# A hybrid attention and state-space layer: who requests the copies of V and the raw weights, and how far apart the convolution and SSD steps stand

## The chip, the cores and the metric

The kernel runs on one core of one Trainium2 chip. The metric is the device time of one execution in microseconds; two runs of the kernel before gave 2359.36 and 2364.16 us, median 2361.76.

## The reference

One decoder layer over 2048 tokens of width 1024, in float32. A projection gives queries, keys, values and a gate for attention, and a gate, an input and the matrices B and C for a state-space mixer:

```python
proj = jnp.einsum('bsd,de->bse', x, w_in[layer])
q, k, v, z_att, z_ssm, xbc, dt_raw = jnp.split(proj, list(SPLITS), axis=-1)
...
o1, l1 = dilated_window_attention(q, k, v, slopes, DILATIONS[0])
o2, l2 = dilated_window_attention(q, k, v, slopes, DILATIONS[1])
o3, l3 = dilated_window_attention(q, k, v, slopes, DILATIONS[2])
...
xbc = jax.nn.silu(causal_depthwise_conv(xbc, conv_w[layer], conv_b[layer]))
xs, bm, cm = jnp.split(xbc, [D_SSM, D_SSM + SSM_GROUPS * SSM_STATE], axis=-1)
...
mix = jnp.concatenate([y_att, y_ssm], axis=-1)
out = jnp.einsum('bse,ed->bsd', mix, w_out[layer])
x = layer_norm(alpha * x + out, ln_g[layer], ln_b[layer])
```

Attention has 16 heads and runs with dilations 1, 4 and 16, so the keys' and values' positions are wanted in three orders. The mixer (SSD) works in 16 chunks of 128 tokens and two groups of heads, so in 32 units, with a causal convolution of width 4 ahead of it and a Silu behind that.

## The kernel before, in words

The engines are called PE (TensorE, matmul), DVE (VectorE), ACT (ScalarE), POOL (GpSimd) and SP (SyncE). SP, ACT and POOL request DMA transfers, each in its own order; a request that has to wait holds up everything behind it on that engine. Matrices are split into a high and a low float32r part, and a product is three matmuls.

**Stage 1, to about 207 us.** V (and the raw time step dt) is computed from `xT`; the rows go to DRAM as `d_v[0]` (`v_out`, L163), dt as `d_dt` (L214). Meanwhile POOL loads the first token side T, 14 tiles of 1 MB.

**Stage 2, 207 to about 1421 us.** All other projections, 44 jobs of two column blocks each. A job is a Strassen-like scheme of seven products (`products`, L283), in the order of the T tiles B11, T1, B21, T2, B22, T4, T3. A product is 12 matmuls into one PSUM bank. ACT evicts four of the seven with `keep` (L297), DVE adds the others to them with `put` (L303, L305). The first ten jobs work on the first half of the tokens (phase 0), the next 22 on the second half (phase 1), the last 12 on the first again (phase 2); at each change all T tiles are loaded anew by POOL (L229). The kinds are c (convolution input), s (SSD gate), q, k and z.

A job's seven weight tiles come from four raw blocks: `column_load` (L234) requests four loads of 256 KB into `wr` tiles (seven buffers), and `column_side` (L241) makes the sums on DVE (L244) and splits each into high (ACT, L248) and low (POOL, L249). The load is requested by POOL, at the seventh step of the job two before the one that uses it; the split runs one job ahead, from its third step on, so that a weight tile is ready five products before it is used.

**What sets the order.** PE, DVE, ACT and POOL follow the program's text. `after(n, f)` puts a piece of work n steps later, and `flush` runs the pieces of a step; a step is one product. SP's order is not the text's: a scheduler sets it from its own estimate of when each request could go.

Pieces that the change touches:

- `copy_v` (L475, request in L478): 32 copies of 512 KB from DRAM to DRAM that write V in the orders of dilations 4 (`d_v[1]`) and 16 (`d_v[2]`). They are entered for every fourth step from step 3 on; attention reads the result from 1421 us on.
- `sums_load` and `sums_part` (L95, L103): in the first four jobs, `xT` is loaded again (L100), DVE and ACT make the sums T1 to T4 of the second token half (L108, L110, L111), and SP stores them (L112). The `to` tiles have two buffers.
- `decays` (L422): loads dt back in 16 small requests (`xr`, L433) and computes the decays, a chain of small operations.
- `conv_tiles` (L370) sets up the two tiles U of a convolution job: SP loads, and a small memset on POOL (L378) that has to wait until the tile's former contents are stored. `conv_fin` (L382) places the five steps of each convolution (`conv_steps`, L390): a scaling on ACT (L395), three taps on DVE (L398), and four Silu pieces on ACT (L404), after which SP stores the result. The first convolution of a job has its steps at 5 to 9, the second at 10 to 14, counted from the job's first step.
- `ssd_load` (L485) and `ssd1` to `ssd5`: per unit, ACT requests `xs`, `bc` and `csb`, two steps ahead of the unit; `ssd5` ends with the gating, and for the first four chunks with a split of the result (L578, L579). `spots` gives each unit its step, every five steps at first and then about every four. `ssd_plan` (L609) enters them all at the first step of job 22.

**Stage 3, from 1421 us.** Attention, then the output projection and the layer norm.

Of the kernel before, what the change touches and what calls it, by code (L numbers as in the profile page):

```python
# [9 lines left out]
F32 = mybir.dt.float32  # L10
# [7 lines left out]
D = 1024  # L18
NR = 16
NJ = 128  # L20
# [8 lines left out]
def hybrid_layer(ctx, tc, xT, xc, w52, wv, convw, convb, dtb, alog, dskp, gcol, wout,  # L29
# [56 lines left out]
    with ExitStack() as c1:  # L86
# [147 lines left out]
        def column_load(ct0, ct1):  # L234

            q = {nm: wr.tile([128, 4, 128], F32, name="wr") for nm in ("S1", "A11", "A12", "A22", "A21")}
            for nm, ct, h in (("A21", ct1, 0), ("A22", ct1, 1), ("A11", ct0, 0), ("A12", ct0, 1)):
                nc.gpsimd.dma_start(q[nm], w52[ct][:, 4 * h:4 * h + 4, :])
            return q
# [130 lines left out]
        def conv_tiles(i):  # L370
            U = []
            for ci in range(2):
                u = cp.tile([128, 19, NJ], F32, name="U", bufs=2)
                for tb in range(2):
                    nc.sync.dma_start(u[:, 3 + tb:19:4, :],
                                      d_cu[i + ci][:, tb].rearrange("p (s j) -> p s j", j=NJ))
                nc.sync.dma_start(u[:, 0, 1:NJ], d_cu[i + ci][:, 1, 3 * NJ:4 * NJ - 1])
                nc.gpsimd.memset(u[:, 0:3, 0:1], 0.0)  # L378
                U.append(u)
            return U  # L380

        def conv_fin(i, U):  # L382
            def f(ci, q, e):
                nc.vector.tensor_copy(U[ci][:, 1 + q, 1:NJ], U[ci][:, 17 + q, 0:NJ - 1])
                if (ci, q) in ((1, 0), (0, 1)):
                    for n, g in enumerate(conv_steps(U[ci], i + ci)):
                        after(n + 3 * ci, g)
            return f
# [86 lines left out]
        def copy_v(d, b):  # L475

            o = (b % 4 * 512 + b // 4 * 32, 8 * b)[d - 1]
            nc.sync.dma_start(d_v[d][b], dap(d_v[0], o * D, [[128 * D, (4, 16)[d - 1]], [D, (32, 8)[d - 1]], [1, D]]))  # L478
# [82 lines left out]
        def ssd5(A):  # L561
# [34 lines left out]
        q = column_load(*cts[0])  # L596
# [7 lines left out]
        q = column_load(*cts[1])  # L604
        units = [(n, g) for n in range(16) for g in range(2)]
        spots = [7 * 22 + 5 + 5 * i if i < 13 else 7 * 32 + (41 * (i - 13)) // 10 for i in range(32)]
        SSD, global_q, sd, H = {}, [None], None, None

        def ssd_plan():  # L609
# [16 lines left out]
        with tc.manual_schedule(engines={E.PE, E.DVE, E.Activation, E.Pool}):  # L626
# [13 lines left out]
            for m, (ph, (kind, i)) in enumerate(jobs):  # L640
# [33 lines left out]
                if m == 22:  # L674
                    after(0, ssd_plan)
# [6 lines left out]
                W, T, q = nW, nT, global_q[0]  # L682
# [536 lines left out]
```

## Time and profile before

| | |
|---|---|
| median of the two runs | 2361.76 us |
| the profiled execution | 2359.14 us, span 2357.3 us, mean granted clock 0.939 |
| PE busy | 2076.8 us, 88% |
| DVE, ACT, POOL busy | 1363.4, 1133.8, 1057.4 us |
| DMA | 557.5 MB, 237 GB/s in the mean |
| POOL on raw weight loads (L238) | 128 requests, 69.1 us |
| ACT waiting for the loads of `csb` (L511) | 69.4 us |

How to read it. Busy PE time says little where matmuls run at half pace, so the granted clock stands beside it, and the time of a stage is compared with the number of its matmuls. "A <- B" means that A sat idle until B ended. A bracket behind a timeline row is the idle time ahead of it and who ended it. SPq, ACTq and POOLq are the requests of DMA transfers; an "issue" as a releaser is time in which the profile shows no cause. All times of a timeline are microseconds from the span's start.

### The profile page before, as it was taken

What the parts mean: (1) busy time and instruction counts of PE and PEld (TensorE: products, weight loads), DVE (VectorE), ACT (ScalarE), POOL (GpSimd) and SP (SyncE); (2) the same over time, 40 slices, a digit from 0 to 9 for tenths busy, and PEclk for the clock granted to TensorE, in tenths of its full rate; (3) what the DMA queues carried; (4) which work ended last, traced back from release to release, by engine and by line L of the source; (5) the groups of instructions that cost most, each with busy time, mean ns of one, the idle gap of its engine ahead of it and who ended that gap; (6) DMA issues with size and microseconds to landing.
All of it is one profiled execution on the core that took longest, in us unless ns stands there. A gap on an engine that the chain in (4) does not pass through costs nothing.

```text
span 2357.3 us, 38953 instructions
## 1 busy us (share of the span) xinstructions
PE 2076.8 (88%) x13824; PEld 1721.2 (73%) x13824; DVE 1363.4 (58%) x3141; ACT 1133.8 (48%) x2969; POOL 1057.4 (45%) x935
## 2 busy tenths in 40 slices
PE   7997148997999788997899997999999996899998
PEld 7997037876777566775678875888788885788886
DVE  3521026435677756773445543888888883666555
ACT  3321025433445456673466644888788882122221
POOL 2122025554556556774444423277666663222221
PEclk9998579999999999998999995999999998899999
DMA  9997376695546788999989984477777779532220
GB/s 334 376 326 300 139 252 216 223 341 199 150 128 213 266 304 318 347 334 390 358 275 303 322 268 160 138 213 221 219 216 228 231 232 315 188 122 89 85 87 35
DMA packets 272882, 557.51 MB, mean 237 GB/s; under 512 B 45360, under 2 KB 136624, under 8 KB 256688
## 3 DMA queue, kind: packets, MB, share of 16 engines
q1 hardware_dynamic: 207200, 308.59, 40.3%
q0 software_dynamic: 44752, 204.49, 24.6%
q10 hardware_dynamic: 20736, 41.95, 5.7%
q8 instruction: 109, 1.79, 0.3%
q14 instruction: 85, 0.70, 0.1%
HBM read 357.42 MB, written 214.30 MB: 243 GB/s over the span
## 4 chain that ended last, share of the span: by engine, by line
PE 41%; DMA 10%; DVE 4%; ACT 3%; issue 1%; POOL 1%; SPq 0%; ACTq 0%; POOLq 0%; DVEq 0%
PE S L785 5%; PE N L834 5%; PE T L814 5%; PE S L994 3%; PE S L996 3%; PE S L995 3%; PE pp L288 3%; PE pp L290 3%; PE pp L292 3%; ACT P L801 2%; PE T L994 2%; DMA bc<-d_bc 2%; PE T L995 2%; PE T L996 2%; DMA kl<-d_kl 1%; DMA wb<-d_wd 1%
## 5 line engine op out<-in xcount | busy, mean ns | idle before, releaser
L249 POOL TENSOR_TENSOR w<-wr,w 128x512 fp32r<-128x512 f32 x224 | 330.9, 1491 | 314.1 <-ACT w L248 310.1
L801 ACT ACTIVATE P<-P,st 128x256 f32<-128x256 f32 (+1 forms) x768 | 345.1, 451 | 96.2 <-DVE st L793 95.5
L793 DVE CUSTOM_DVE_ANT_0 P<-S,tb 128x256 f32<-128x256 f32 (+1 forms) x768 | 235.1, 362 | 98.7 <-PE S L785 66.5
L816 DVE COPY PT<-T 128x512 f32<-128x512 f32 (+1 forms) x304 | 196.5, 677 | 1.5 <-PE T L814 1.5
L297 ACT COPY ev<-pp 128x512 f32<-128x512 f32 x176 | 102.4, 582 | 182.8 <-PE pp L292 145.8
L814 PE MATMUL T<-ident,P 128*128 128x128 f32 x1200 | 179.5, 287 | 5.9 <-DVE PT L816 5.9
L248 ACT CAST w<-wr 128x512 fp32r<-128x512 f32 x224 | 136.5, 619 | 93.6 <-DMA wr<-w 49.3
L834 PE MATMUL N<-PT,v 128*64 128x128 f32 x2400 | 176.6, 284 | 0.0
L244 DVE TENSOR_TENSOR wr<-wr 128x512 f32<-128x512 f32 x128 | 134.5, 1051 | 51.8 <-DMA wr<-w 31.6
L305 DVE TENSOR_TENSOR ev<-pp,ev 128x512 f32<-128x512 f32 x152 | 100.7, 682 | 92.4 <-PE pp L292 72.6
L834 PEld LDWEIGHTS N<-PT,v 128*64 128x64 f32 x2400 | 129.3, 138 | 33.3 <-issue 22.6
L814 PEld LDWEIGHTS T<-ident,P 128*128 128x128 f32 x1200 | 130.0, 142 | 30.8 <-DVE PT L816 7.3
L288 PE MATMUL pp<-TT3h,w 128*128 128x512 f32 x176 | 73.6, 418 | 83.1 <-ACT ev L297 83.0
L801 ACT ACTIVATION_READ_ACCUMULATOR P<-P,st 128x1 f32 x768 | 143.8, 187 | 0.0
L901 POOL TENSOR_TENSOR wb<-num,wb 128x2048 f32<-128x2048 f32 x21 | 96.4, 4591 | 97.0 <-DMA wb<-d_wd 83.6
L785 PE MATMUL S<-kh,qp 64*128 64x256 f32 (+1 forms) x1024 | 126.5, 306 | 0.0
L971 DVE TENSOR_REDUCE tb<-P 128x128 f32<-128x1024 f32 x32 | 64.0, 1999 | 84.9 <-PE N L1000 49.2
L511 ACT ACTIVATE mt<-csb,cs 128x128 f32<-128x128 f32 x256 | 78.4, 390 | 70.7 <-DMA csb<-d_cs 69.4
L345 DVE SCALAR_TENSOR_TENSOR ev<-ev 128x512 f32<-128x512 f32 x64 | 64.0, 1015 | 77.2 <-ACT ev L344 77.2
L288 PE MATMUL pp<-TB22h,w 128*128 128x512 f32 x176 | 77.0, 437 | 35.5 <-ACT ev L297 35.4
L785 PEld LDWEIGHTS S<-kh,qp 64*128 64x128 f32 x1024 | 88.9, 188 | 22.0 <-issue 21.0
L288 PEld LDWEIGHTS pp<-TT3h,w 128*128 128x128 f32 x176 | 34.8, 197 | 95.1 <-ACT ev L297 87.3
(362 smaller groups left out, 6110.5 us busy)
## 6 DMA issues: line engine op xcount, KB each, us to landing
d_wc<-w SPq DMA_DIRECT2D x84, 512.0 KB
w<-d_wc POOLq DMA_DIRECT2D x84, 512.0 KB, 7.4
wr<-w POOLq DMA_DIRECT2D x128, 256.0 KB, 4.9
v<-d_v POOLq DMA_DIRECT2D x24, 1024.0 KB, 7.0
wb<-d_wd SPq DMA_DIRECT2D x48, 512.0 KB
csb<-d_cs ACTq DMA_DIRECT2D x32, 512.0 KB
st<-xT SPq DMA_DIRECT2D x31, 512.0 KB
d_v<-vt SPq DMA_DIRECT2D x16, 512.0 KB
```

What stands on the lines that cost most here:

```text
L244: tt = lambda o, a, b, op=OP.subtract: nc.vector.tensor_tensor(q[o], q[a], q[b], op=op)
L248: nc.scalar.copy(t[:, 0], q[nm])
L249: nc.gpsimd.tensor_tensor(t[:, 1], q[nm], t[:, 0].bitcast(F32), op=OP.subtract)
L288: nc.tensor.matmul(ps, w[:, 0, k], th[:, k], start=start and k == 0, stop=False, skip_group_check=not start)
L785: nc.tensor.matmul(ov(sp[h][:, 256 * b:256 * b + w]), A["q"][d][x][hr, blk], kv(A["k"][y][hr]), start=(m == 0), stop=(m == 2))
L793: nc.vector.tensor_tensor_reduce(P[:, h, b, 256 - w:256], sp[h][:, c0:c0 + w], tab[:, h, tab.shape[2] - w:], 1.0, 3.0e38, OP.add, OP.min, ...
L801: nc.scalar.activation(p, p, AF.Exp, bias=stat(A, 0, d, h, blk), scale=-1.0, accum_out=stat(A, 1, d, h, blk))
L814: nc.tensor.transpose(tp[:, h, b], P[:, h, b, 128 * which:128 * which + 128], ident)
L816: nc.vector.tensor_copy(pt[:, :, bl[0]:2], tp[:, :, bl[0]:2])
L834: nc.tensor.matmul(nm[64 * h:64 * h + 64, bq * 128:bq * 128 + 128], v[:, k, 64 * h:64 * h + 64], pts[which][:, h, b], start=(f or not whic ...
L994: nc.tensor.matmul(ps, uh[:, e, :], wh, start=(e == 0), stop=False)
L995: nc.tensor.matmul(ps, uh[:, e, :], wl, start=False, stop=False)
```

## The change

1. `copy_v` is requested by ACT instead of SP, so that it stands where the text puts it.
2. `column_load` inside the loop over jobs (30 jobs, 120 requests) is requested by ACT instead of POOL, and in four pieces, at steps 3, 4, 6 and 7 of the job, in the order A11, A12, A22, A21, instead of all four at step 6 in the order A21, A22, A11, A12. The loads of the first two jobs stay on POOL.
3. Each convolution's Silu stands two steps behind its last tap instead of one, and the second convolution's steps stand at 11, 12, 13, 14 and 16. The second U tile of a job is set up three steps after the first.
4. The SSD units start two steps later, at a spacing of 63/13 of a step instead of 5 for the first 13; their loads stand three steps ahead of the unit instead of two; the split of the first chunks' result becomes a step of its own (`ssd6`), one later. `ssd_plan` is entered three steps later.

```diff
-        def column_load(ct0, ct1):
-
-            q = {nm: wr.tile([128, 4, 128], F32, name="wr") for nm in ("S1", "A11", "A12", "A22", "A21")}
-            for nm, ct, h in (("A21", ct1, 0), ("A22", ct1, 1), ("A11", ct0, 0), ("A12", ct0, 1)):
-                nc.gpsimd.dma_start(q[nm], w52[ct][:, 4 * h:4 * h + 4, :])
-            return q
+        def column_load(ct0, ct1, queue=nc.gpsimd):
+
+            q = {}
+
+            def load(nm, ct, h):
+                q[nm] = wr.tile([128, 4, 128], F32, name="wr")
+                queue.dma_start(q[nm], w52[ct][:, 4 * h:4 * h + 4, :])
+
+            def first():
+                q["S1"] = wr.tile([128, 4, 128], F32, name="wr")
+                load("A11", ct0, 0)
+            return q, [first, lambda: load("A12", ct0, 1), lambda: load("A22", ct1, 1), lambda: load("A21", ct1, 0)]
...
-        def conv_tiles(i):
-            U = []
-            for ci in range(2):
-                u = cp.tile([128, 19, NJ], F32, name="U", bufs=2)
...
+        def conv_tile(i, U):
+            u = cp.tile([128, 19, NJ], F32, name="U", bufs=2)
...
-                        after(n + 3 * ci, g)
+                        after((0, 1, 2, 3, 5)[n] + 4 * ci, g)
...
-            nc.sync.dma_start(d_v[d][b], dap(d_v[0], o * D, [[128 * D, (4, 16)[d - 1]], [D, (32, 8)[d - 1]], [1, D]]))
+            nc.scalar.dma_start(d_v[d][b], dap(d_v[0], o * D, [[128 * D, (4, 16)[d - 1]], [D, (32, 8)[d - 1]], [1, D]]))
...
             nc.sync.dma_start(d_us[g][n], xd)
+
+        def ssd6(A):
+            n, g, xd = A["n"], A["g"], A["xd"]
             if n < 4:
...
-        spots = [7 * 22 + 5 + 5 * i if i < 13 else 7 * 32 + (41 * (i - 13)) // 10 for i in range(32)]
+        spots = [7 * 23 + 63 * i // 13 if i < 13 else 7 * 32 + (41 * (i - 13)) // 10 for i in range(32)]
...
-                after(max(0, n0 - 2 if i else 0), lambda i=i: load(i))
-                for d, f in ((0, ssd1), (1, ssd2), (2, ssd3), (3, ssd4), (4, ssd5)):
-                    after(n0 + d + (i == 0), lambda i=i, f=f: f(SSD[i]))
+                after(n0 - 3, lambda i=i: load(i))
+                for d, f in ((0, ssd1), (1, ssd2), (2, ssd3), (3, ssd4), (4, ssd5), (5, ssd6)):
+                    after(n0 + d, lambda i=i, f=f: f(SSD[i]))
...
-                    def load(m=m):
-                        global_q[0] = column_load(*cts[m + 2])
-                    after(6, load)
+                    q2, steps_ = column_load(*cts[m + 2], nc.scalar)
+                    for n, f in zip((3, 4, 6, 7), steps_):
+                        after(n, f)
...
-                    after(0, lambda i=i, U=U: U.extend(conv_tiles(i)))
+                    after(0, lambda i=i, U=U: conv_tile(i, U))
+                    after(3, lambda i=i, U=U: conv_tile(i + 1, U))
...
-                    after(0, ssd_plan)
+                    after(3, ssd_plan)
```

In the built programs the instructions then stand as follows. SP, where stage 1 ends and stage 2 begins; `d_v_100` is V as computed, `d_v_101` and `d_v_102` the two copies, `st` the loads of `xT`, `d_T1T` the stores of the sums:

```order
 L163 DMA d_v_100<-vt 128x4x256
-L478 DMA d_v_101<-d_v_100 4x2x16384 x4
-L426 DMA dtbt<-dtb 128x16
-L428 DMA al<-alog 128x16
-L433 DMA xr<-d_dt 8x16x16 x16
+L428 DMA dtbt<-dtb 128x16
+L430 DMA al<-alog 128x16
+L435 DMA xr<-d_dt 8x16x16 x16
 L100 DMA st<-xT 128x1024 x2
-L478 DMA d_v_101<-d_v_100 4x2x16384 x4
-L478 DMA d_v_102<-d_v_100 16x8192 x16
 L112 DMA d_T1T_119<-to 128x2x512
```

Before, eight more copies stand three rows further up. Now all 32 have left SP; between the last store of V and the load of `xT` stand only the decay inputs.

ACT in phase 0, after the change, some steps of jobs 0 and 1 (L303 is `keep`, L254 the high part of a weight, L110 the cast of a sum, L240 a raw weight load, L480 a copy of V):

```order
L240 DMA wr<-w 128x512
L110 CAST to<-st 128x512
L303 COPY ev<-pp 128x512
L254 CAST w<-wr 128x512 x2
L240 DMA wr<-w 128x512
L303 COPY ev<-pp 128x512
L480 DMA d_v_101<-d_v_100 4x2x16384
L254 CAST w<-wr 128x512
L240 DMA wr<-w 128x512
```

Before, none of these requests stood on ACT here. They now stand between evictions that PE waits for.

ACT at the end of a job's second convolution, before (L297 is `keep`, L404 the Silu pieces, L356 the Silu of the gate):

```order
L356 ACTIVATE ez<-ev 128x4x16x8
L248 CAST w<-wr 128x512
L297 COPY ev<-pp 128x512
L248 CAST w<-wr 128x512
L404 ACTIVATE U<-acc,cb 128x4x16x8 x4
L356 ACTIVATE ez<-ev 128x4x16x8 x2
L297 COPY ev<-pp 128x512
```

and after (L303 `keep`, L406 the Silu pieces, L362 the Silu of the gate):

```order
L362 ACTIVATE ez<-ev 128x4x16x8 x2
L303 COPY ev<-pp 128x512
L254 CAST w<-wr 128x512
L406 ACTIVATE U<-acc,cb 128x4x16x8 x4
L254 CAST w<-wr 128x512
L303 COPY ev<-pp 128x512
L480 DMA d_v_102<-d_v_100 16x8192
```

Before, the gate's Silu and the next eviction stand behind the convolution's four pieces; now they stand ahead of them, and what follows the pieces is the eviction of a later product.

More of the change, by code (lines that the diff above doesn't have):

```diff
@@ L368, in fin_u @@
             return f
-        def conv_tiles(i):
-            U = []
-            for ci in range(2):
-                u = cp.tile([128, 19, NJ], F32, name="U", bufs=2)
[L374 to L380, printed above, removed]
+        def conv_tile(i, U):
+            u = cp.tile([128, 19, NJ], F32, name="U", bufs=2)
+            for tb in range(2):
+                nc.sync.dma_start(u[:, 3 + tb:19:4, :], d_cu[i][:, tb].rearrange("p (s j) -> p s j", j=NJ))
+            nc.sync.dma_start(u[:, 0, 1:NJ], d_cu[i][:, 1, 3 * NJ:4 * NJ - 1])
+            nc.gpsimd.memset(u[:, 0:3, 0:1], 0.0)
+            U.append(u)
         def conv_fin(i, U):
@@ L595, in hybrid_layer @@
         T, steps = token_side(0)
-        q = column_load(*cts[0])
+        q, steps_ = column_load(*cts[0])
+        for f in steps_:
+            f()
         W, prep = column_side(q)
@@ L603, in hybrid_layer @@
             f()
-        q = column_load(*cts[1])
+        q, steps_ = column_load(*cts[1])
+        for f in steps_:
+            f()
         units = [(n, g) for n in range(16) for g in range(2)]
-        spots = [7 * 22 + 5 + 5 * i if i < 13 else 7 * 32 + (41 * (i - 13)) // 10 for i in range(32)]
-        SSD, global_q, sd, H = {}, [None], None, None
+        spots = [7 * 23 + 63 * i // 13 if i < 13 else 7 * 32 + (41 * (i - 13)) // 10 for i in range(32)]
+        SSD, sd, H, q2 = {}, None, None, None
         def ssd_plan():
@@ L681, in hybrid_layer @@
                 products(W, T, fin, to)
-                W, T, q = nW, nT, global_q[0]
+                W, T, q = nW, nT, q2
                 if m in (1, 2, 3):
```

## The prediction

> **What bounds the kernel now.** I read the page's slices first, to see where TensorE (PE) is not the limit; one slice is 58.9 us.
>
> ```profile
> PE   7997148997999788997899997999999996899998
> PEclk9998579999999999998999995999999998899999
> ```
>
> The fifth and sixth slices (236 to 354 us) are nearly empty and run at a low clock. From the fourteenth on there are shallower holes, and from 1436 us on (attention and output) nothing that the diff touches. So I took the busy time by stretch, then the timeline of PE with the idle time ahead of a matmul in brackets, for the start of the projections and for the convolutions.
>
> ```profile
> 195.00:207.00 12.00, 9.09 (x73) 8.88 (x72) 2.33 (x12) 1.35 (x4) 2.88 (x6) 0.98 1.10 427
> 227.20:252.00 24.80, 0.01 (x1) 0.00 (x0) 0.00 (x0) 0.00 (x0) 0.00 (x0) 0.56 0.24 100
> 252.00:279.00 27.00, 0.00 (x0) 0.00 (x0) 0.00 (x0) 0.00 (x0) 0.00 (x0) 0.50 0.25 85
> 375.00:500.00 125.00, 125.00 (x549) 103.34 (x549) 63.38 (x82) 62.55 (x111) 77.63 (x77) 0.99 0.74 243
> 588.79:829.81 241.02, 204.52 (x841) 164.93 (x841) 167.37 (x137) 113.40 (x181) 138.58 (x119) 0.92 0.62 192
> 850.00:1075.00 225.00, 206.19 (x1088) 169.57 (x1085) 163.31 (x227) 144.72 (x294) 152.63 (x136) 0.98 0.92 330
> ...
> 207.71 0.80 PE L288 MATMUL pp<-TB11h,w 128*128 128x512 f32 x1 [3.61 <-ACT w L248]
> 287.92 0.79 PE L288 MATMUL pp<-TT3h,w 128*128 128x512 f32 x1 [60.72 <-ACT ev L297]
> 328.95 0.77 PE L288 MATMUL pp<-TB21h,w 128*128 128x512 f32 x1 [30.72 <-DVE ev L305]
> 345.66 0.50 PE L288 MATMUL pp<-TT3h,w 128*128 128x512 f32 x1 [3.50 <-ACT ev L297]
> 374.11 0.79 PE L288 MATMUL pp<-TT3h,w 128*128 128x512 f32 x1 [7.46 <-ACT ev L297]
> ...
> 548.88 0.79 PE L288 MATMUL pp<-TT3h,w 128*128 128x512 f32 x1 [6.38 <-ACT ev L297]
> 588.79 0.79 PE L288 MATMUL pp<-TB22h,w 128*128 128x512 f32 x1 [3.88 <-ACT ev L297]
> 634.57 0.79 PE L288 MATMUL pp<-TB22h,w 128*128 128x512 f32 x1 [3.87 <-ACT ev L297]
> 680.29 0.50 PE L288 MATMUL pp<-TB22h,w 128*128 128x512 f32 x1 [3.83 <-ACT ev L297]
> 829.81 0.79 PE L288 MATMUL pp<-TB22h,w 128*128 128x512 f32 x1 [13.07 <-ACT ev L297]
> ```
>
> The columns of a stretch are its length, the busy time of PE, PE's weight loads, VectorE (DVE), ScalarE (ACT) and GpSimd (POOL), the granted clock, the DMA share and GB/s. From 375 to 500 us PE never waits: 549 matmuls in 125 us, 0.228 us each, so a product of 12 costs 2.73 us. By this measure 207.71 to 374.11 holds 20 products, 54.6 us of work in 166.4: 112 us are lost, 92 of them in two gaps. Between 548.88 and 829.81 stand 82 products, 224 us in 281: 57 us are lost, in gaps before TB22 and in the matmuls at half pace behind each gap (0.79 us against 0.50).
>
> Who holds the two large gaps? The waits of that stretch, and SyncE's (SP's) own order:
>
> ```profile
> DVE st L108 <- DMA st<-xT: 68.5, 1, 68.5
> ACT to L110 <- DMA d_T1T<-to: 38.5, 1, 38.5
> ...
> 206.73 0.41 DVE L75 COPY vt<-ss 128x256 f32<-128x256 f32 x1
> 281.61 0.69 DVE L108 TENSOR_TENSOR st<-st 128x512 f32<-128x512 f32 x1 [68.49 <-DMA st<-xT]
> ...
> 195.05 14.11 SPq L478 DMA_DIRECT2D d_v<-d_v  x8
> 222.18 0.36 SPq L163 DMA_DIRECT2D d_v<-vt  x1
> 252.03 2.44 SPq L478 DMA_DIRECT2D d_v<-d_v  x4
> 255.54 22.54 SPq L433 DMA_DIRECT2D xr<-d_dt  x16
> 278.18 0.83 SPq L100 DMA_DIRECT2D st<-xT  x2
> 279.06 35.31 SPq L478 DMA_DIRECT2D d_v<-d_v  x20
> 315.29 0.38 SPq L112 DMA_DIRECT2D d_T1T<-to  x1
> ...
> SPq L478 <- DMA d_v<-vt: 52.3, 3, 29.4
> SPq L478 <- DMA d_v<-d_v: 24.6, 12, 5.4
> ```
>
> PE needs an eviction by ACT, ACT stands at a cast of the sums (L110), that waits for DVE, and DVE for `xT`. The load of `xT` is requested only at 278.18, behind 12 copies of V. The second gap is the mirror: the store of the sums (L112) is requested at 315.29, behind 20 more copies, and the two `to` buffers are full until it lands. The DMA is not the bound: its share is 0.24 and 0.25 while everything stands still. The first eight copies keep a quarter of the DMA engines busy, and the last store of V, requested at 222.18, took until 252.03 to land. The Trainium skill (DMA: Bandwidth & Descriptors, "Why a DMA increments its semaphore by 16 and not by 1") says that a transfer is spread over as many engines as divide its slowest dimension, 4 here; the shares of 0.24 and 0.25 agree.
>
> **The change part by part.** *Copies of V off SP.* In the new order SP goes from the last store of V straight to the decay inputs, the load of `xT` and the sums' stores. When does `xT` land? DVE writes the last piece of V at 206.73 to 207.1. Its store, or that of dt beside it, lands between 3.4 us later (as `xT` did, 278.18 to 281.61) and 29.4 (the row above, behind copies that are now gone); I take 12, since the DMA carried 427 GB/s until 207 and must drain. The 16 loads of `xr` took 22.54 us behind four copies; by their median request of 0.32 us they take 5.2, and with one landing 8.6, which I take. Then 3.4 for `xT`, and 6.3 from DVE's L108 to PE's matmul (281.61 to 287.92). The sum from 207.1 is 12 + 8.6 + 3.4 + 6.3 = 30.3, so PE goes on at 237 and its gap is 10 instead of 60.7: 50 saved. The bounds are 60.7 (3.4 + 5.2 + 3.4 + 6.3 ends before PE gets there) and 19 (29.4 + 22.5 + 3.4 + 6.3). Of the second gap I keep 3 for a store's landing: 28 saved, bounds 20 and 31. The gap of 3.5 goes with it, since POOL's weight loads were late for the same reason, and 3 of the half-pace matmuls. The 7.46 stays: DVE is then in the chain for the decays. Together **84 us**, bounds 40 and 98.
>
> *What the copies cost on ACT.* Each request takes 0.56 us, one in four products (10.9 us), beside casts already running:
>
> ```profile
> L478 SPq DMA_DIRECT2D d_v<-d_v x32: 467/562/753, 195.1 to 313.9; - x32
> L238 POOL DMA_DIRECT2D wr<-w x112 | 60.3, 543 | 9.7 <-DMA TT2h<-d_T1T 2.7 <-DMA TB22l<-d_T1B 2.3 <-DMA TB22h<-d_T1B 2.2
> L489 ACTq DMA_DIRECT2D xs<-d_xs x32: 326/446/1555, 819.6 to 1380.2; - x32
> 914.81 0.62 ACT L248 CAST w<-wr 128x512 fp32r<-128x512 f32 x1 [7.44 <-DMA d_kh<-ev]
> ```
>
> From 375 to 500 us ACT is busy for 62.55 of 125, so that hides; if it did not, the 32 requests would be 18 us. A copy also shares four engines for about 5 us (the longest wait of one copy for another is 5.4), less than the two products before a weight is wanted. I charge 2 us, bounds 0 and 10. At the change of the T tiles (548.88) the weights no longer stand behind 14 MB on POOL's queue, which may give back the 6.38, but three or four copies at 1.8 us each (35.31 over 20) now run there: zero, bounds -6 and +8.
>
> *Convolutions further apart.* In today's order the four Silu pieces (L404) stand one step after the last tap, and the eviction that PE needs stands behind them:
>
> ```profile
> 673.75 2.33 DVE L398 SCALAR_TENSOR_TENSOR acc<-U,cw,acc 128x2048 f32<-128x2048 f32 x1
> 676.17 2.56 ACT L404 ACTIVATE U<-acc,cb 128x512 f32<-128x512 f32 x4 [4.14 <-issue]
> 679.67 0.56 ACT L297 COPY ev<-pp 128x512 f32<-128x512 f32 x1
> 638.46 0.10 POOL L378 MEMSET U<- 128x3 f32 x1 [6.91 <-issue]
> 828.20 0.33 ACTq L491 DMA_DIRECT2D bc<-d_bc  x1
> ```
>
> ACT stands 4.14 us until the tap of 673.75 is done, works 2.56, and only then evicts at 679.67; PE starts at 680.29. With one step more between, the tap has 2.73 us more and the eviction goes first, so the 3.8 to 3.9 us gap of each pair of jobs should close, with the half pace behind it. The 13.07 at 829.81 is the first load of B and C waiting on ACT (until 828.20) for the last convolution's store; it moves from the same step as that convolution's Silu to two steps behind it. DVE's own work is no new bound: 167.37 us for five pairs that need 191 of PE. POOL's wait of 6.91 for a freed U stays about as long (the Silu now stands one step ahead of the next tile instead of none, but is 2.56 us long and its store must land), and its weights are wanted only five products, 13.6 us, after their step. Of the 57 us I take back 41 and give 7 to new waits of ACT: 120 weight loads now stand in ACT's order, each behind a buffer that POOL or DVE must release. **34 us**, bounds -10 and 50.
>
> *The state-space units.* Loads go one step earlier, the split of the result one step later. In 850 to 1075 PE is idle 19 of 225 us, so no more than that can be won. Against it: ACT is busy for 145 of 225 and gets 32 weight loads in its order, in a stretch with a DMA share of 0.92. The nearest rows for a request that waits are 2.05 us (24.6 over 12 on SP) and 7.44 (ACT at 914.81, held by an earlier transfer); 32 by 2.05 is 66 us against 80 idle. Most hides; where it bunches, PE waits. I charge **10 us**, bounds -15 and +66 (nothing hidden).
>
> *Sum.* -84 + 2 + 0 - 34 + 10 = -106 on the profiled span of 2357.3 gives 2251; with the 1.8 us around the span (2359.14 for that execution) 2253. The two runs shown have their median at 2361.76, 2.6 above, so on the scale of the runs the forecast is **2255 us**.
>
> **The rivals.** *The waits move to ACT* (first rival). ACT now waits for POOL's release four times a job, the convolution stretch gives nothing, the units cost 25 and the start gives 75: 2361.8 - 75 + 25 = 2312. For it: ACT already stood 7.44 us at one request. Against: ACT has half its time free until 825 us, and PE runs two products ahead of it.
>
> *Only the request's time is saved* (second rival). The bytes are the same and 32 copies of 0.5 MB read and write as much as before; if the transfers and not their order held the sums, only SP's 32 requests of 0.56 us would be gained, 18 us: 2344. The Trainium skill has this rule (DMA: Bandwidth & Descriptors, "Issuing engines are not separate DMA queues"): transfers requested on several engines run on the same 16 DMA engines, and only the requesting engine's own time is saved. Against it stand the shares of 0.24 and 0.25 in the gap; the trace shows an order, not a lack of bandwidth.
>
> *ACT becomes the bound* (the other side). The place is 375 to 1075 us: 152 requests enter an order where ACT is idle for about half, 350 of 700 us. At 2.05 us each with a request of 0.45 they take 380 and use that up; from about 2.5 us on each further microsecond costs 152. At 4 us they take 676, some 326 more than is free; half of it beside gaps of PE that are there anyway leaves +163, against the -84 of the start: 2361.8 + 79 = 2441. For it: 7.44, and a landing of 29.4 beside copies. Against: the copies come singly now, and most loads wait on something two or more products old.
>
> That the change does not do what it says is excluded for the copies by the new order of SP, which holds none.
>
> **How the numbers follow.** The forecast (2215 to 2300) has 0.70, ACT's waits (2312) 0.20, the request's time alone (2344) 0.05, ACT as the bound (2441) 0.05. The 8 in 10 go from 2212, where the start, the convolutions and the units all do better than taken, to 2315, which takes in the first rival. Two per cent, about what a measurement of this kernel can tell from no change, is 47 us, a time of 2314. Faster: the forecast and three quarters of the first rival, 0.85. Within: the rest of that and the second, 0.10. Slower: 0.05.
>
> **What would show it.** Right: `xT` requested before 235 us, PE's gap of 60.7 below 20, none of 30 after it; the 374.11 matmul near 290; pairs of convolution jobs at 38 to 41 us instead of 45.7; no wait of ACT for L404 above 2 us. Wrong at the start: a gap above 40 there although SP holds no copy. Wrong at the convolutions: pairs still at 45, with ACT idle ahead of a weight request. The third rival would show as ACT waiting in sum over 100 us on requests between 375 and 1075 us, with PE waiting for ACT's eviction.

## The result, and the profile after

| | before | after |
|---|---|---|
| median of the runs | 2361.76 us (2359.36 to 2364.16) | 2278.78 us (2278.00 to 2279.57) |
| ratio, with its 95% interval | 1 | 0.9649 (0.9604 to 0.9693) |
| span of the profiled execution, mean granted clock | 2357.3 us, 0.939 | 2277.8 us, 0.948 |
| PE busy | 2076.8 us, 88% | 2088.7 us, 92% |

The changed kernel saves 83 us where 107 were forecast. Line numbers of the changed kernel are mostly 6 higher than those of before (L297 is now L303, L244 is L250, L249 is L255). First the page's slices, 56.9 us each now:

```profile
PE   7999789879898899988999979999999985999998
PEclk9999889989999999998999978999999997999999
```

The two empty slices are gone. In their place stand sevens, eights and nines up to the fourteenth slice (to 797 us): less than a hole, more than nothing. Next the timelines of the changed kernel, of SP's requests, of DVE's first sum, and of PE with the idle time ahead of a matmul:

```profile
208.95 0.38 SPq L163 DMA_DIRECT2D d_v<-vt  x1
211.20 13.83 SPq L435 DMA_DIRECT2D xr<-d_dt  x16
225.13 0.84 SPq L100 DMA_DIRECT2D st<-xT  x2
230.84 0.38 SPq L112 DMA_DIRECT2D d_T1T<-to  x1
...
228.69 0.69 DVE L108 TENSOR_TENSOR st<-st 128x512 f32<-128x512 f32 x1 [12.62 <-DMA st<-xT]
...
235.01 0.80 PE L294 MATMUL pp<-TT3h,w 128*128 128x512 f32 x1 [5.67 <-ACT ev L303]
262.77 0.79 PE L294 MATMUL pp<-TT3h,w 128*128 128x512 f32 x1 [6.13 <-ACT ev L303]
291.04 0.80 PE L294 MATMUL pp<-TT3h,w 128*128 128x512 f32 x1 [6.89 <-ACT ev L303]
391.09 0.80 PE L294 MATMUL pp<-TT2h,w 128*128 128x512 f32 x1 [3.99 <-ACT ev L303]
435.20 0.80 PE L294 MATMUL pp<-TT2h,w 128*128 128x512 f32 x1 [3.03 <-ACT ev L303]
451.56 0.80 PE L294 MATMUL pp<-TT3h,w 128*128 128x512 f32 x1 [5.07 <-ACT ev L303]
...
705.68 0.80 PE L294 MATMUL pp<-TB22h,w 128*128 128x512 f32 x1 [4.31 <-ACT ev L303]
```

`xT` is requested at 225.13 instead of 278.18, the gap of 60.7 is 5.67, the one of 30.7 does not exist. But the forecast read 375 to 500 us as a stretch without any wait of PE, and there stand now gaps of 3 to 5 us, with matmuls at 0.80 us behind them.

For the account, the span is cut at the first matmul on TB11 of jobs 0, 3, 11, 23, 32 and 43, read from PE's timeline of each kernel (before, these stand at 207.7, 379.1, 554.2, 841.0, 1082.1 and 1399.9 us). Jobs 0 to 3 are the start of stage 2, 3 to 11 the rest of phase 0 with the change of the T tiles, 11 to 23 hold the convolutions, 23 to 32 the state-space units, 32 to 43 is phase 2; the remainder up to the span's end is stage 3 with the last job. This table is used below for every experiment; the medians and ratios of the experiments come from other chips than the kernel before's 2361.76, so ratios are each against the kernel before on the same chip. e10 is the changed kernel run a second time; its columns differ from those of "after" by at most 2.0 us, which tells how far a column can be trusted.

| kernel | 0 to 3 | 3 to 11 | 11 to 23 | 23 to 32 | 32 to 43 | rest |
|---|---|---|---|---|---|---|
| before | 171.4 | 175.1 | 286.8 | 241.1 | 317.8 | 957.4 |
| after | 86.8 | 200.6 | 264.2 | 243.0 | 313.0 | 960.9 |
| e1 copies only | 83.1 | 200.4 | 290.2 | 242.1 | 315.4 | 957.9 |
| e2 loads only | 172.4 | 170.5 | 291.0 | 233.0 | 318.4 | 958.5 |
| e3 steps only | 171.5 | 176.2 | 252.1 | 250.5 | 309.9 | 959.4 |
| e4 all but the copies | 171.5 | 173.2 | 260.5 | 242.9 | 318.6 | 958.4 |
| e5 copies late | 77.9 | 170.6 | 294.8 | 247.4 | 313.4 | 959.8 |
| e6 copies over 16 rows | 79.0 | 176.7 | 264.7 | 240.8 | 312.9 | 959.4 |
| e7 second U later | 87.2 | 200.7 | 241.2 | 244.9 | 318.8 | 958.4 |
| e8 four wot buffers | 86.2 | 196.9 | 264.4 | 243.1 | 310.4 | 960.9 |
| e9 e6 and e7 | 79.3 | 177.2 | 239.9 | 240.4 | 312.0 | 958.2 |
| e10 the change again | 87.2 | 200.5 | 264.2 | 243.0 | 315.0 | 961.3 |
| e11 copies over 2 rows | 99.3 | 257.5 | 261.6 | 243.7 | 312.2 | 960.5 |
| e12 units' places only | 173.1 | 176.4 | 279.9 | 243.9 | 312.9 | 957.2 |

After against before: -84.6 in the start, +25.5 in jobs 3 to 11, -22.6 in the convolutions, +1.9 in the units, -4.8 and +3.5 behind them. Two numbers need a cause: the 25.5 that are given back, and the 11 missing from the convolutions. The waits of the changed kernel from 290 to 500 us, the largest and those for `wot`:

```profile
POOL w L255 <- ACT w L254: 96.3, 30, 16.7
DVE wot L118 <- ACT wot L117: 51.1, 14, 12.1
ACT wot L117 <- DMA d_wo<-wot: 44.8, 8, 12.5
PE pp L294 <- ACT ev L303: 21.9, 5, 6.9
ACT w L254 <- DMA d_cu<-ev: 19.1, 1, 19.1
DVE wr L250 <- DMA wr<-w: 9.0, 4, 3.0
```

The columns are the sum, the number and the longest of the waits. ACT stands 44.8 us for a store: `wot` (L117) is the prepared output weight, made in phase 0, with two buffers; `split_w` fills one, SP stores it to `d_wo`, and the next needs the store landed. PE waits for ACT's eviction behind it: three of its four waits for an eviction in jobs 3 to 11 (3.99, 3.03 and 5.07 above) follow a wait of ACT for such a store, of 8.68, 8.09 and 12.47 us. The last of them, on ACT:

```profile
449.80 0.72 ACT L117 ACTIVATE wot<-woraw,gc 128x512 fp32r<-128x512 f32 x1 [12.47 <-DMA d_wo<-wot]
...
450.94 0.57 ACT L303 COPY ev<-pp 128x512 f32<-128x512 f32 x1
```

PE starts at 451.56. In the kernel before the same operation never waited for its store. What makes the store late?

### The profile page after: what moved, and what is told of

It is laid out like the page before. It is cut to its first block, busy times and chain, and to the rows that moved or that the text cites. A ratio compares the mean times of both kernels' runs of the same rounds, so it can differ in the third digit from the quotient of the medians.

```text
span 2277.8 us, 38897 instructions
## 1 busy us (share of the span) xinstructions
PE 2088.7 (92%) x13824; PEld 1729.8 (76%) x13824; DVE 1368.8 (60%) x3141; ACT 1132.2 (50%) x2967; POOL 1017.3 (45%) x815
## 3 DMA queue, kind: packets, MB, share of 16 engines
q1 hardware_dynamic: 206496, 291.81, 39.8%
## 4 chain that ended last, share of the span: by engine, by line
PE 40%; DMA 12%; DVE 5%; ACT 4%; issue 2%; POOL 1%; ACTq 0%; SPq 0%; DVEq 0%; POOLq 0%
PE S L795 6%; PE N L844 6%; PE T L824 6%; PE S L1004 3%; PE S L1006 3%; PE S L1005 3%; DMA zt<-d_zs 3%; PE pp L294 2%; PE pp L296 2%; PE pp L298 2%; PE T L1004 2%; PE T L1005 2%; PE T L1006 2%; ACT P L811 1%; DVE P L803 1%
## 5 line engine op out<-in xcount | busy, mean ns | idle before, releaser
L255 POOL TENSOR_TENSOR w<-wr,w 128x512 fp32r<-128x512 f32 x224 | 354.3, 1599 | 282.4 <-ACT w L254 223.2
L303 ACT COPY ev<-pp 128x512 f32<-128x512 f32 x176 | 102.2, 581 | 156.4 <-PE pp L298 103.6
L250 DVE TENSOR_TENSOR wr<-wr 128x512 f32<-128x512 f32 x128 | 129.9, 1015 | 71.9 <-POOL w L255 54.0
L254 ACT CAST w<-wr 128x512 fp32r<-128x512 f32 x224 | 136.2, 618 | 62.7 <-DVE wr L250 21.2
L844 PEld LDWEIGHTS N<-PT,v 128*64 128x64 f32 x2400 | 129.3, 138 | 33.3 <-issue 22.6
L400 DVE SCALAR_TENSOR_TENSOR acc<-U,cw,acc 128x2048 f32<-128x2048 f32 x36 | 106.6, 2961 | 6.0 <-ACT acc L397 5.5
L146 PE MATMUL pp<-vh,xh 128*128 128x256 f32 (+1 forms) x320 | 90.8, 290 | 14.5 <-ACT xh L169 14.5
```

Of the source, the lines that this page charges most:

```text
L250: tt = lambda o, a, b, op=OP.subtract: nc.vector.tensor_tensor(q[o], q[a], q[b], op=op)
L254: nc.scalar.copy(t[:, 0], q[nm])
L255: nc.gpsimd.tensor_tensor(t[:, 1], q[nm], t[:, 0].bitcast(F32), op=OP.subtract)
L844: nc.tensor.matmul(nm[64 * h:64 * h + 64, bq * 128:bq * 128 + 128], v[:, k, 64 * h:64 * h + 64], pts[which][:, h, b], start=(f or not whic ...
```

## Experiments

**e1, e2, e3, e4: the parts alone.** e1 has only the first edit (copies of V on ACT), e2 only the second (weight loads on ACT), e3 only the third and fourth (steps), e4 everything but the first.

```diff
 e1, on the kernel before
-            nc.sync.dma_start(d_v[d][b], ...
+            nc.scalar.dma_start(d_v[d][b], ...
 e4, on the changed kernel
-            nc.scalar.dma_start(d_v[d][b], ...
+            nc.sync.dma_start(d_v[d][b], ...
```

> The kernel before with one part of the change: the copies of V are requested by ScalarE. Theory: the copies' place in SyncE's order held the sums of the second token half, so the fourth job starts some 83 us earlier (379.06 us before, about 296 here), and the copies, which then run beside the stores of the output weights, cost about 25 us up to the change of the T tiles: about 2303 us in all. Rival: the 26 us lost there come from the raw weight loads on ScalarE; then nothing is given back and the time is about 2278 us.

> The kernel before with one part of the change: the raw weight loads of 30 jobs are requested by ScalarE, in four pieces. Theory: they cost and bring little, 2355 to 2368 us, and the jobs of phase 0 after the fourth run without a gap, as before. Rival (the loads on ScalarE are what costs 26 us in phase 0): 2380 to 2390 us, with waits of ScalarE on them between 375 and 500 us.

> The kernel before with one part of the change: the convolution and SSD steps stand further apart. Theory: the 23 us won between the jobs 11 and 23 come from these steps, so about 2336 us, with pairs of convolution jobs near 44 us. Rival: they come from GpSimd being free of the weight loads; then about 2360 us and pairs at 45.7 us.

> The changed kernel with the copies of V back on SyncE. Theory: the two large gaps (60.7 and 30.7 us) are back, phase 0 runs without a gap after them, and the convolution jobs are as in the changed kernel: about 2335 us. Rival (the loads on ScalarE cost the 26 us of phase 0): about 2361 us.

| | median | ratio (95%) |
|---|---|---|
| e1 copies only | 2306.78 us | 0.9745 (0.9725 to 0.9765) |
| e2 loads only | 2357.42 us | 0.9963 (0.9948 to 0.9978) |
| e3 steps only | 2334.04 us | 0.9864 (0.9845 to 0.9883) |
| e4 all but the copies | 2332.67 us | 0.9853 (0.9826 to 0.9880) |

e1 settles where the 25.5 come from: with no weight load and no step moved, jobs 3 to 11 take 200.4 us against 175.1. It is the copies, not the 120 loads that ACT got; e2 and e4, which have these loads, take 170.5 and 173.2 there. e3 takes 34.7 off the convolutions, the forecast's 34; with the loads beside it (e4) it is 26.3, in the whole change 22.6. The parts multiply to 0.958, and the whole has 0.963 (e10, below): they seem to get in each other's way by about 12 us (7 to 10 by the profiled spans), though the intervals leave some 9 us open.

The Trainium skill (DMA: Bandwidth & Descriptors, "Issuing engines are not separate DMA queues") says that requesting on another engine saves only the requester's time. e1 moves 32 requests of 0.56 us, 18 us by that rule, and saves 60: the measurement goes beyond the rule, and what it adds is the work that stood behind requests that waited.

**e5: the same copies, 74 steps later.**

```diff
-                later.setdefault(4 * j + 3, []).append(lambda j=j: copy_v(1 + j // 16, j % 16))
+                later.setdefault(4 * j + 77, []).append(lambda j=j: copy_v(1 + j // 16, j % 16))
```

> The changed kernel with the 32 copies of V entered 74 places later (places 77 to 201 instead of 3 to 127), still on ScalarE's queue. The changed kernel took 0.965 of the kernel before; 26 us of its start were given back between the products that begin at 296 and at 497. Theory: the copies of V, running beside the prepared output weights, keep their stores from landing, and ScalarE waits for the two buffers. Without copies there the give-back goes: products 3 to 11 keep 80 us or more of the start, and the convolutions, which now have the copies beside them, lose 0 to 12: ratio 0.955 to 0.960, 2255 to 2268 us beside 2362. Rival: the give-back comes from what the earlier start itself puts closer together (raw weights, stores of xs and U in the same stretch); then products 3 to 11 still lose about 25 and the ratio stays at 0.965 or rises.

2274.03 us, ratio 0.9597 (0.9577 to 0.9617). Jobs 3 to 11 take 170.6: the give-back is gone, and ACT's wait for `wot` with it (0.5 us). The rival falls. But jobs 11 to 23, which now have the copies over 4 rows beside them, take 294.8, 30.6 more than in the changed kernel, where I expected 12 at most: the cost moved with the copies. It belongs to them and not to phase 0. What is late there seems to be another store: POOL stands up to 11.5 us at the memset of a U, against 5.3 in the changed kernel.

**e6: the same bytes at the same steps, over 16 rows instead of 4.** V's order of dilation 4 takes four runs of 32 rows. As written, the slowest dimension is 4; nothing forbids cutting each run into 16 pieces and walking the pieces first.

```diff
-            nc.scalar.dma_start(d_v[d][b], dap(d_v[0], o * D, [[128 * D, (4, 16)[d - 1]], [D, (32, 8)[d - 1]], [1, D]]))
+            if d == 1:
+                nc.scalar.dma_start(dap(d_v[d], b * 128 * D, [[2 * D, 16], [32 * D, 4], [1, 2 * D]]),
+                                    dap(d_v[0], o * D, [[2 * D, 16], [128 * D, 4], [1, 2 * D]]))
+            else:
+                nc.scalar.dma_start(d_v[d][b], dap(d_v[0], o * D, [[128 * D, 16], [D, 8], [1, D]]))
```

> The changed kernel with the first 16 copies of V written as 64 pieces of 16 KB over 16 rows instead of 4 pieces of 64 KB; the same bytes move at the same places. Theory that a copy of 4 pieces occupies 4 of the 16 DMA engines for long and makes every other transfer with a share on these engines late: ScalarE's waits for wot (44.8 us in 8 waits) fall below 20, phase 0 gives back under 12 instead of 26, ratio 0.956 to 0.961 (2258 to 2270 us). Rival, that it is the number of copies and their place in time, or the count of requests, whatever their shape: waits and ratio unchanged (0.963 to 0.967).

(The sizes in that text are wrong. The page counts 16193 packets of 8 KB or more for the changed kernel and 17089 for this one, 56 more for each of 16 copies: 8 packets of 64 KB became 64 of 8 KB.)

2245.53 us, ratio 0.9489 (0.9470 to 0.9507), 33 us better than the change, and better than the theory asked for. Jobs 3 to 11 take 176.7 (1.6 given back instead of 25.5), and the start gains another 7.8. The waits of this kernel from 290 to 500 us:

```profile
DVE wot L118 <- ACT wot L117: 26.1, 11, 5.3
ACT w L254 <- DMA d_cu<-ev: 15.2, 1, 15.2
ACT wot L117 <- DMA d_wo<-wot: 11.3, 5, 3.7
```

44.8 us have become 11.3, and in jobs 3 to 11 PE waits for no eviction any more, where it waited 15.0 us in the changed kernel.

**e11: the same packets, over 2 rows.** e6 changes two things, the rows and the size of a packet. Here the 8 packets of 64 KB stay (16193 packets of 8 KB or more, as in the changed kernel) and only the outermost count is 2.

```diff
-                nc.scalar.dma_start(dap(d_v[d], b * 128 * D, [[2 * D, 16], [32 * D, 4], [1, 2 * D]]),
-                                    dap(d_v[0], o * D, [[2 * D, 16], [128 * D, 4], [1, 2 * D]]))
+                nc.scalar.dma_start(dap(d_v[d], b * 128 * D, [[16 * D, 2], [32 * D, 4], [1, 16 * D]]),
+                                    dap(d_v[0], o * D, [[16 * D, 2], [128 * D, 4], [1, 16 * D]]))
```

> The changed kernel with the first 16 copies of V in the same 8 packets of 64 KB, but written with 2 rows outermost instead of 4. Theory that the outermost count sets over how many DMA engines a copy is spread: alone, a copy then shows a DMA share of about 0.13 instead of 0.26, everything else with a part on these two engines is later still, the waits for wot grow beyond 44.8 us and the ratio is 0.970 or more (2291 us). Rival, that the size of the packets or their number does it and not the spread: share 0.26, ratio 0.960 to 0.966 as in the changed kernel.

2348.09 us, ratio 0.9920 (0.9902 to 0.9939): nearly the whole gain of the change is eaten. Jobs 3 to 11 take 257.5, 82.4 given back. Three stretches in which little but a copy moves, of the changed kernel (4 rows), of e11 (2) and of e6 (16, with other transfers beside); the last two columns are the DMA share and GB/s:

```profile
244.00:247.00 3.00, 3.00 (x15) 2.49 (x14) 1.40 (x3) 1.70 (x4) 0.35 (x1) 1.00 0.26 104
```

```profile
245.00:247.00 2.00, 2.00 (x11) 1.57 (x9) 0.00 (x0) 0.00 (x0) 0.00 (x0) 1.00 0.11 41
```

```profile
236.00:240.00 4.00, 4.00 (x15) 3.23 (x14) 3.01 (x4) 0.26 (x1) 1.71 (x2) 0.76 1.02 357
```

A quarter, about an eighth, and all of the engines. At 104 GB/s a copy of 512 KB keeps its engines for 5.0 us of every 10.9 us between copies; at 41 GB/s for 12.8, and at the 50 GB/s from 248 to 250 us (share 0.13) for 10.5, which is about all the time there is. The Trainium skill (DMA: Bandwidth & Descriptors, "Why a DMA increments its semaphore by 16 and not by 1") takes the number of engines from the slowest dimension and counts a transfer as landed when the last engine has its share; the shares of 0.26, 0.11 and 1.02 agree with the first half. From the second half, a store that has a share on a busy engine ends only there. That fits the first stores beside a copy: ACT's cast of the sums needs a buffer back from one of them, and waits the longer the fewer rows the copy has (4 rows, 2 rows, 16 rows):

```profile
244.95 0.62 ACT L110 CAST to<-st 128x512 fp32r<-128x512 f32 x1 [7.93 <-DMA d_T1T<-to]
```

```profile
248.00 0.62 ACT L110 CAST to<-st 128x512 fp32r<-128x512 f32 x1 [12.56 <-DMA d_T1T<-to]
```

```profile
240.04 0.62 ACT L110 CAST to<-st 128x512 fp32r<-128x512 f32 x1 [3.79 <-DMA d_T1T<-to]
```

The stretch of 0.11 (245 to 247 us) lies inside the second wait: the store was unfinished while most engines were idle. It fits the waits for `wot` in e11 as well, from 290 to 500 us:

```profile
ACT wot L117 <- DMA d_wo<-wot: 59.7, 7, 13.9
ACT to L110 <- DVE st L108: 39.2, 5, 20.1
DVE wr L250 <- DMA wr<-w: 29.7, 3, 16.1
```

e11 shows that the rows alone do it, from 4 to 2. From 4 to 16 the packets became smaller too, and no run parts the two.

**e8: four buffers for `wot`.**

```diff
-                after(3, lambda: split_w(j // 2, j % 2, raw, sums.tile([128, 2, 512], F32R, name="wot", bufs=2)))
+                after(3, lambda: split_w(j // 2, j % 2, raw, sums.tile([128, 2, 512], F32R, name="wot", bufs=4)))
```

> The changed kernel with four buffers instead of two for the prepared output weights (wot); copies, loads and order as in the changed kernel. Theory that the late landing of their stores is paid only through ScalarE's wait for one of the two buffers: with four the waits of 44.8 us fall below 15, phase 0 gives back under 12 instead of 26, ratio 0.956 to 0.961 (2258 to 2270 us). Rival, that the transfers are late for everything and the next thing in line (token sums, evictions, TB tiles) waits instead: ratio 0.963 to 0.967.

2268.56 us, ratio 0.9581 (0.9567 to 0.9596). The ratio lies where the theory wanted it, but the trace sides with the rival: ACT's wait for the store falls to 0.8 us, and jobs 3 to 11 still give back 21.8 us. The waits from 290 to 500 us:

```profile
ACT w L254 <- DMA d_cu<-ev: 29.2, 3, 13.0
DVE wr L250 <- DMA wr<-w: 20.4, 5, 9.6
ACT wot L117 <- DMA d_wo<-wot: 0.8, 1, 0.8
```

The first two were 19.1 and 9.0 us above, but the changed kernel's second profile (e10) has 25.3 and 18.5, so their growth is not shown. PE's own waits in jobs 3 to 11 say more, first in the changed kernel, then in e8:

```profile
PE pp L294 <- ACT ev L303: 15.0, 4, 5.1
PE pp L296 <- DMA TB21l<-d_T1B: 4.0, 1, 4.0
```

```profile
PE pp L294 <- ACT ev L303: 7.3, 3, 3.1
PE pp L294 <- DMA TB11h<-d_T1B: 3.1, 1, 3.1
```

In sum PE waits 7.3 us for evictions (15.0, and 18.5 in e10) and 19.5 us for loads of T tiles (13.2, and 13.3 in e10). By the starts of the jobs, jobs 3 to 9 give back 16.1 us instead of 26.2, and job 10, where the T tiles change, gives back 5.8 where the changed kernel gained 0.6. So the wait for `wot` was worth about 10 us, and more than half of that came back where the T tiles are loaded. What makes up the 16.1 was not taken apart.

**e7: the second U two steps later.** For the 11 us that the convolutions lack, the waits of three pairs of convolution jobs (535 to 668 us) in the changed kernel:

```profile
ACT U L406 <- DVE acc L400: 33.2, 6, 6.9
DVE wr L250 <- POOL w L255: 25.2, 9, 6.2
PE pp L294 <- ACT ev L303: 10.1, 6, 2.2
```

and how one of them comes about, from the timelines of POOL, DVE, ACT and PE of the same kernel:

```profile
670.26 0.10 POOL L381 MEMSET U<- 128x3 f32 x1 [5.32 <-issue]
670.46 2.53 POOL L255 TENSOR_TENSOR w<-wr,w 128x512 fp32r<-128x512 f32 x2
...
671.78 1.76 DVE L250 TENSOR_TENSOR wr<-wr 128x512 f32<-128x512 f32 x1 [6.29 <-POOL w L255]
673.46 0.22 DVE L386 COPY U<-U 128x127 f32<-128x127 f32 x1
...
673.76 2.01 ACT L397 ACTIVATE acc<-U,cw 128x2048 f32<-128x2048 f32 x1 [7.62 <-DVE U L386]
676.18 0.58 ACT L303 COPY ev<-pp 128x512 f32<-128x512 f32 x1
...
676.81 0.50 PE L294 MATMUL pp<-TT2h,w 128*128 128x512 f32 x1 [1.18 <-ACT ev L303]
```

POOL stands 5.32 us at the memset of the second U, whose buffer is still being stored (this row names no cause; the same wait at 538.48 and at 625.57 us ends with the store `d_xs<-U`); behind it is the low half of a weight (L255), so DVE gets no `wr` buffer for 6.29, the convolution's tile is late, ACT waits 7.62 at the scaling, and the eviction that PE needs stands behind the scaling.

```diff
-                    after(3, lambda i=i, U=U: conv_tile(i + 1, U))
+                    after(5, lambda i=i, U=U: conv_tile(i + 1, U))
```

> The changed kernel with the second conv tile set up two places later (place 5 instead of 3). Theory that GpSimd's wait for the second U, ahead of its share of the weights, makes VectorE wait for weight buffers (49.0 us in 17 waits) and so costs the convolutions the 11 us missing from their 34: VectorE's wait for L255 falls below 25 us, four conv pairs take 41 to 42 us instead of 43.9, ratio 0.958 to 0.962 (2262 to 2272 us). Rival, that the second U is then late for its own products and the wait only moves to ScalarE's or GpSimd's tap accumulation: ratio 0.963 to 0.968.

2256.59 us, ratio 0.9531 (0.9508 to 0.9554), more than expected. Jobs 11 to 23 take 241.2, 23 less than in the changed kernel; a pair takes 39.7 us (after 44.1, before 46.2, from the starts of jobs 13 and 19). The same place in e7:

```profile
660.07 0.10 POOL L381 MEMSET U<- 128x3 f32 x1 [1.12 <-DMA d_xs<-U]
...
657.73 1.76 DVE L250 TENSOR_TENSOR wr<-wr 128x512 f32<-128x512 f32 x1 [1.19 <-POOL w L255]
```

The wait is shorter, and it now comes behind DVE's sums, not ahead of them. With the second U at the same step, the wait is 2.0 to 2.6 us with the steps alone (e3), 3.3 to 4.3 with the weight loads on ACT beside them (e4), and 3.4 to 5.3 in the changed kernel, which has the copies there too. By what path the loads and copies lengthen it was not tried and stays open.

**e12: the units' places alone.**

```diff
-        spots = [7 * 22 + 5 + 5 * i if i < 13 else 7 * 32 + (41 * (i - 13)) // 10 for i in range(32)]
+        spots = [7 * 23 + 63 * i // 13 if i < 13 else 7 * 32 + (41 * (i - 13)) // 10 for i in range(32)]
...
-                after(max(0, n0 - 2 if i else 0), lambda i=i: load(i))
-                for d, f in ((0, ssd1), (1, ssd2), (2, ssd3), (3, ssd4), (4, ssd5)):
-                    after(n0 + d + (i == 0), lambda i=i, f=f: f(SSD[i]))
+                after(n0 - 3, lambda i=i: load(i))
+                for d, f in ((0, ssd1), (1, ssd2), (2, ssd3), (3, ssd4), (4, ssd5), (5, ssd6)):
+                    after(n0 + d, lambda i=i, f=f: f(SSD[i]))
```

> The kernel before with the new placing of the SSD units alone (units at other places, the pieces' last part one place later, loads three places ahead); copies, loads of weights and conv tiles as before. The prediction counted this at 10 us lost: ratio 1.002 to 1.007, the products from 841 to 1082 us together some 10 us longer. Rival, that ScalarE's wait for the mixed tile (30.7 us in 8 waits before, 6.0 after) was on the path: ratio 0.987 to 0.996.

2356.07 us, ratio 0.9950 (0.9934 to 0.9966). By the ratio the rival holds, by the trace neither: jobs 23 to 32 take 243.9, 2.8 more than before, and the gain lies ahead of them, at the last convolution. There PE's timeline in e12 has

```profile
827.17 0.80 PE L288 MATMUL pp<-TB22h,w 128*128 128x512 f32 x1 [6.92 <-ACT ev L297]
```

against 13.07 before (at 829.81): the first load of B and C is further from the last Silu. The forecast had this gain, but under the convolutions; some 7 of the 34.7 us of e3 are this.

**e10 and e9: the change again, and both edits that helped.** e9 is the changed kernel with the edits of e6 and e7; e10 is the changed kernel unedited, on the same chip.

> The changed kernel once more, unedited, so that the ratios of the edits stand beside its own on this chip: 0.960 to 0.966. Outside that range the differences of the edits from it have to be worked out anew.

> The changed kernel with both edits that helped alone: the first 16 copies of V over 16 rows (alone 0.9489) and the second conv tile set up two places later (alone 0.9531). Theory that they are two costs at two places, the stores beside the copies before 497 us and GpSimd's share of the weights after it, so that they add: with the changed kernel at 0.960 to 0.965, ratio 0.937 to 0.944 (2213 to 2230 us beside 2362), and the product that begins at 1082 in the kernel before begins 120 us or more earlier instead of 78. Rival, that one takes the place of the other (the DMA engines or the clock set the pace once one is gone): 0.946 to 0.950.

e10: 2282.00 us, ratio 0.9627 (0.9605 to 0.9649). e9: 2222.51 us, ratio 0.9388 (0.9370 to 0.9406), 60 us below the change and 145 below the kernel before. The two edits alone take 0.0138 and 0.0096 off 0.9627, which makes 0.9393: they add, so they are two costs at two places. Jobs 3 to 11 take 177.2, the convolutions 239.9, and among the waits of e9 in these jobs (467 to 707 us) are

```profile
ACT U L406 <- DVE acc L400: 35.4, 10, 5.5
DVE wr L250 <- POOL w L255: 16.0, 11, 2.7
```

The last was 39.8 us, with a longest wait of 6.3, in the same jobs of the changed kernel.

## Why the prediction was right, and where it was off

The result lies inside the range, on its upper half, and the forecast's own case held: the start and the convolutions gain, the units cost little. Two terms were too good by 23.5 and 11.4 us and one too bad by 8.1; that the last took back part of the first two is luck. By the terms of the sum, on the profiled spans:

| term | forecast | measured | shown by |
|---|---|---|---|
| start of stage 2 | -84 | -84.6 | e1: -88.3 |
| copies on ACT in phase 0, and the T tiles' change | +2 (0 to +10), and 0 (-6 to +8) | +25.5 | e1, e5, e6, e11 |
| convolutions | -34 (-10 to 50 saved) | -22.6 | e3, e7 |
| state-space units | +10 | +1.9 | e2, e12 |
| phase 2, rest, and ahead of job 0 | 0 | +0.3 | |
| sum | -106 | -79.5 | |

- **The start** was right in mechanism and in its sum. `xT` requested before 235: 225.13. The gap of 60.7 below 20: 5.67. None of 30 after it. The matmul of 374.11 near 290: 291.04. Inside the sum two terms missed and cancelled, which is luck: 12 us were taken for the landing of V's last store, but SP went on at 211.20, 4 us behind 207.1; 8.6 were taken for the loads of `xr`, and SP stood 13.83 us at them. The gap of 3.50, which was to go, is 6.13; the 7.46, which was to stay, is 6.89. e6 gains 7.8 us more in the start, so part of what is left was the copies' doing too.
- **The copies on ACT** are the mis-sized term, and the step that failed reads "A copy also shares four engines for about 5 us ... less than the two products before a weight is wanted. I charge 2 us". The 5 us were right (5.0 at 104 GB/s). Wrong was the question: I asked who wants a load, and not which store must land before its buffer is free. The 25.5 are some 26 in jobs 3 to 9 and -0.6 in job 10, so the zero for the change of the T tiles held and the whole miss is this step. `wot` has two buffers, takes a new tile every 1.75 products, and ACT, which evicts for PE, stands behind it; with four buffers (e8) 21.8 us are still given back, in part at the loads of the T tiles. The trace of before had a warning, which the prediction itself used for the start: V's store requested at 222.18 landed at 252.03, behind a pile of eight copies. What one copy in every 10.9 us does to a store it could not show, since PE mostly stood still while the copies ran; e1, e5, e6 and e11 do.
- **The convolutions** had the right cause and two thirds of the 34. With the steps alone the term is 34.7 (e3); the loads on ACT take 8.4 of it (e4; the forecast gave them 7, out of 41), the copies 3.7. The failed step: "POOL's wait of 6.91 for a freed U stays about as long ..., and its weights are wanted only five products, 13.6 us, after their step." The wait did stay; but what is behind it on POOL holds the `wr` buffers that DVE needs at once, and through DVE and ACT it reaches PE. Without it (e7) the term is -45.6, and a pair takes 39.7 us, in the range of 38 to 41 that I had named; in the changed kernel it takes 44.1. The sign "no wait of ACT for L404 above 2 us" was wrong: ACT waits up to 6.9 us for the last tap in the changed kernel and 5.5 in e9, though pairs are short there, because the evictions now stand ahead of the Silu.
- **The units**: I charged 10 us for 32 loads that join ACT's order. By e2 these loads gain 8.1 there, and the new places cost 2.8 (e12) to 9.4 (e3, with the convolutions' steps). The sum came out near nothing for other reasons than mine.
- **The rivals.** ACT's waits (2312): what ACT waited longer for were stores in phase 0, 44.8 us, and not the release of a weight buffer ahead of its own requests, which the rival named; that is not among its larger waits. The request's time alone (2344): e1 saves 60 us. ACT as the bound (2441): nothing of it.

## What to carry to other kernels

When a transfer between DRAM tensors is moved beside other work, look at its outermost count first: the same sixteen copies of 512 KB at the same steps cost 82 us in jobs 3 to 11 over 2 rows, 25 over 4 and 2 over 16 (there in smaller packets). When a wait is left where it is because nothing on its engine is wanted soon, follow what that engine's next instructions release, buffers too, and not only what they make. And price a shared resource by the waits for stores that free buffers as well as by loads.

## What was not expected of the hardware

- A DRAM to DRAM copy of 512 KB ran at 104 GB/s with a DMA share of 0.26 over 4 rows and at about 41 GB/s with 0.11 over 2 rows; over 16 rows the stretch with a copy in it carried 357 GB/s at 1.02.
- A copy that keeps few engines busy delays transfers that it shares no queue with: the copies are requested by ACT, and the stores that land late (`d_wo`, `d_T1T`) by SP. In jobs 3 to 11 the mean DMA share of the changed kernel is 0.80 while ACT waits for stores; with 16 rows it is 0.91, with 2 rows 0.63:

```profile
296.10:496.80 200.70, 172.39 (x677) 137.49 (x676) 78.68 (x95) 72.14 (x127) 84.64 (x73) 0.90 0.80 284
```

```profile
289.80:466.60 176.80, 161.32 (x677) 130.53 (x676) 73.36 (x95) 72.22 (x126) 82.54 (x73) 0.95 0.91 319
```

```profile
309.10:566.60 257.50, 180.98 (x676) 141.89 (x675) 81.83 (x97) 71.63 (x127) 84.13 (x73) 0.83 0.63 221
```

  (the changed kernel, e6, e11). Share times length is about 161 us in all three: the same transfers, which take longer the fewer engines a copy has. A DMA share below 1 was here no sign that a transfer had room.
